# A new constant table of turns for the planner of a one-core hybrid decoder layer

## The chip, the cores and the metric

The kernel runs on one core of a Trainium2 chip. Its time is that of one execution on the device, in microseconds (us); the median of three runs is given. The engines are TensorE (PE, with its weight loads shown apart as PEld), VectorE (DVE), ScalarE (ACT), GpSimd (POOL) and SyncE (SP), which issues the DMA transfers. Each takes its instructions in the order in which the program lists them and waits at an instruction until what it needs is there.

## The reference

One layer of a decoder with two groups of heads side by side, for 1024 tokens of width 1024:

```
h = rms_norm(x)
[a_q a_k a_v a_z a_b a_a | b_q b_k b_v b_z i_q i_k i_w] = h @ w_in
A: q,k,v = silu(causal_conv4(a_qkv)); q,k = l2_norm
   g = -exp(a_log) * softplus(a_a + dt_bias); beta = sigmoid(a_b)
   o_a = rms_norm(gated_delta_rule_chunked(q,k,v,g,beta)) * silu(a_z)      4 heads of 128, chunks of 64
B: score[t,s] = sum_h i_w[t,h] * relu(i_q[t,h] . i_k[s]), causal           8 index heads of 128
   keep the 256 best keys per row; softmax attention on them, QK-normed    8 heads of 64, 2 key heads
   o_b = that * silu(b_z)
x = x + concat(o_a, o_b) @ w_out
gate = sigmoid(rms_norm(x) @ w_ple_gate + b)
x = x + (p @ w_ple) * gate
```

In the chunked delta rule each chunk needs cumulative sums of g, and the inverse of a unit triangular matrix `a_mat`, which comes from solving against the identity. All is float32.

## The kernel before

Products in float32 are made of three fast ones: each operand is split into a high part that the fast format holds and the low rest, and `mm3` (L785) adds high·high, high·low and low·high in one PSUM bank. So a weight block of 128x512 is loaded by a DMA (`raww`), its high part `hiw` is a copy on ACT, and its low part `low` a subtraction on POOL. A 128-column block of the input projection, or of the output projection, takes 8 or 4 weight blocks and is one job of the class Stream. In the trace `hTh` and `hTl` are the split parts of h, `mch` and `mcl` those of the concatenated heads.

The work comes in stages that overlap. First the norm of x and the gate values. `gates` (L1011) computes `g` from the small projection: `gu` on DVE, `nea` (an exponential) and three steps of `ge` on ACT, then two steps of `g` on DVE; then two small matmuls on PE give its cumulative sums and totals, which DVE copies to `gg`.

Then, from about 85 to 540 us, the blocks of the input projection fill PE, and between them run: the index scores; the search of the 256 best keys, bit by bit, on DVE (`topk_v`, L1217, with counts into `junk`) and on ACT (`topk_a`, L1254, counts into `junka`, with small updates on POOL); and group A head by head. For each head `merge` (L1607) builds the inverse of 8 chunk pairs of 128x128 from 32x32 blocks in steps: a product of 64 tiny matmuls, a copy of its result to SBUF (`W0`, on ACT), the next product with it, and so on.

Then the sparse attention, and from about 620 us the output projection. `out_job` (L2011) has four sets of jobs: oA and oB for the first 512 tokens, oC and oD for the others, A and C for the first four weight blocks, B and D for the last four. A job of oD fills one of five PSUM banks (tag `g`), DVE adds the residual from x, ACT squares and copies, POOL adds the squares to `ssum`, and `gate_in` (L2091) or `h2` (L2016) splits the result times the gain for the gate product: high part on ACT, low part on DVE or POOL. `m0Bh` and `m0Bl` are such parts of the second half of the features for the first 512 tokens: the high part is an ACT copy of x2 times the gain, the low part the DVE operation `x2 * g - hi` of L2019, whose two tensor operands both lie in SBUF. `h1Al` is the same for the other tokens, with x in PSUM. The gate product itself (`gate_weights`, `gate_pair`, `gate_last`, L2123 to L2225) uses seven block products in place of eight, which needs sums and differences of weights and of h (`mixl`, `sh`, `sl`, `t1l`), many of them on POOL. The last part of the kernel is this product with its output.

What sets the order is a table. The whole layer is first run against the class Plan (L373), which records each call of an engine as an operation, 7,654 of them, 348 being marks for pools and tiles: 3,873 on PE (a run of small matmuls into one tile is one operation), 1,280 on DVE, 1,075 on ACT, 700 on POOL and 378 DMAs on SP. `add` notes which operation must come before which, by tiles and regions. Buffers are chosen in this recording, so they do not depend on the order. Then `run` (L487) decodes the constant string `TURNS` (L76): entry k is the position, in the list of operations not yet taken, of the one that comes next.

```
for k in raw[:len(ops)] + 256 * raw[len(ops):].astype(int):
    o = ops[left.pop(k)]
    assert all(p in seen for p in o.pre)
```

`issue` (L536) writes the instructions in that order; each is tied to the one before it on its engine, so the table is the program order of every engine. All instructions are issued by one line, so all carry L556 in the profile, and groups are told apart by the names of their tiles.

Of the kernel before, what the change touches and what calls it, by code (L numbers as in the profile page):

```python
# [20 lines left out]
T = 1024  # L21
D = 1024
# [25 lines left out]
_o = 0  # L48
# [24 lines left out]
RG, SG = 3, 3  # L73
# [7 lines left out]
Nug69t5L3%BSFw9wOW-%qf)3;qEab{q8JH;g-|Gj<bi-7BqSiY&nI~0GLK-F$?R66Of(_ALd(n5b}>P%=4~pKMWv$kN=`J1YEdsLMNuO`sa64nWKM(%xr$|3;5N$T22Rim
P(~{mPRq$T6({3(PA-=Vl#F9Jj&m{^hGG7UkxWqvyTYKjqtGZ6DuqIneAZsl(n?AtR|;~4LP5v{nFP`(^(AyX!Ldq~6{Ue>EXzsPMclW^5iHZ!$1ofzRkAcg(=@dR#|Kbe
Uiq$s%J01UH-wS+!4JRl<8Oca-S4TD^6xvo-_-ui@Be_~4Mr247+BJPuWalesDG&W%1@l0uiNlny54sEBFpuaul=LT^=6g}xBNLC$BlT}t2iFTUkMu{Mx!xkyrT^maQx|K
a2)sCQsKB`0bjuJtNb&#ng0@hf#-S6Ii4%zPMzZLIvf{@a6A*w$jG=Pbto)}73?gE#|z^5@x00S(Rjs7MMcGU#U<%)1kc8^mK@9~Syxh0f^RvxrFa70+&?a%Xl&P5#^~yi
# [2274 lines left out]
```

## Time and profile before

| what | value |
|---|---|
| median of three runs | 832.26 us (831.86, 832.26, 835.58) |
| profiled execution | 835.29 us, span 833.3 us |
| mean granted clock of PE | 0.984 |
| PE busy | 811.9 us (97%), 5063 instructions |
| DVE busy | 664.9 us (80%) |
| ACT busy | 589.6 us (71%) |
| POOL busy | 540.9 us (65%) |
| DMA | 93.14 MB |

The span is the part of the profiled execution in which instructions ran. A line of the timeline gives the start, the duration, the engine, the line, the operation, `out<-in` by the program's names, the shapes and a count; in brackets stands how long the engine had stood idle before, and what it waited for. Matmuls overlap in the pipeline, so the time that one costs is read between the starts of two, not from its duration. The clock is the share of full speed granted to PE. The page's clock row and engine rows cut the span into 40 slices of 20.8 us and give tenths.

### The profile page before, as it was taken

The page shows a single profiled execution, that of the slowest core. Times are in us where ns is not written, and L with a number is a line of the kernel's source. Part 1 is how long each engine was busy: PE and PEld are TensorE (multiplying, and loading weights), DVE is VectorE, ACT ScalarE, POOL GpSimd, SP SyncE. Part 2 cuts the span into 40 slices and gives each one's busy share as a digit, 9 for nine tenths or more (in the row PEclk, how much of TensorE's full clock was granted, in tenths as well). Part 3 has the DMA queues.
Part 4 walks back from the last instruction along what each step waited for, and adds up shares of the span by engine and source line. Part 5 has one row for each costly group of instructions (what it writes and reads, how often), then busy time and mean ns, then how long its engine had stood idle before and what let it go on. Part 6 is the DMA issues. An engine that isn't in the chain of part 4 may idle for free.

```text
span 833.3 us, 14829 instructions
## 1 busy us (share of the span) xinstructions
PE 811.9 (97%) x5063; PEld 692.2 (83%) x5063; DVE 664.9 (80%) x1475; ACT 589.6 (71%) x1345; POOL 540.9 (65%) x704
## 2 busy tenths in 40 slices
PE   9998999999999999999999999999999999979996
PEld 6996999987888888888888888878888888768885
DVE  3698757888999999998768854699998786586676
ACT  5765466667999989999775543499886678765342
POOL 3487667524876677577748545368675647988982
PEclk9998999999999999999899999999999999989999
DMA  8963421001122233113312332676313421522453
GB/s 276 371 241 103 159 85 64 1 13 52 39 70 62 89 84 106 58 52 96 87 52 76 87 91 70 219 218 209 113 51 103 155 71 53 197 94 64 140 172 130
DMA packets 77868, 93.14 MB, mean 112 GB/s; under 512 B 24000, under 2 KB 40672, under 8 KB 77664
## 3 DMA queue, kind: packets, MB, share of 16 engines
q1 hardware_dynamic: 77792, 92.20, 34.4%
q8 instruction: 39, 0.64, 0.3%
q14 instruction: 37, 0.30, 0.1%
HBM read 66.72 MB, written 25.45 MB: 111 GB/s over the span
## 4 chain that ended last, share of the span: by engine, by line
PE 80%; DVE 9%; ACT 6%; issue 2%; DMA 1%; POOL 1%; SPq 0%; DVEq 0%; ACTq 0%
PE mm L556 44%; PE g L556 8%; PE lg L556 6%; PE s L556 5%; PE pv L556 4%; PE S L556 4%; PE pt L556 3%; PE c L556 3%; PE rec L556 2%; ACT junka L556 2%; PE po L556 2%; DVE c L556 1%; DVE xT L556 1%; DVE score L556 1%; DVE g L556 1%
## 5 line engine op out<-in xcount | busy, mean ns | idle before, releaser
L556 PE MATMUL mm<-hThi,hiw 128*128 128x512 f32 x400 | 156.8, 405 | 0.6 <-ACT fst L556 0.3
L556 PE MATMUL mm<-hTlo,hiw 128*128 128x512 f32 x400 | 156.3, 402 | 0.0
L556 PE MATMUL mm<-hThi,low 128*128 128x512 f32 x400 | 155.4, 401 | 0.0
L556 POOL TENSOR_TENSOR low<-raww,hiw 128x512 fp32r<-128x512 f32 (+1 forms) x93 | 123.7, 1335 | 43.0 <-ACT hiw L556 26.4
L556 ACT ACTIVATE junka<-score,nt 128x768 bf16<-128x768 int16 (+5 forms) x96 | 99.7, 1039 | 2.5 <-POOL scr L556 0.4
L556 PEld LDWEIGHTS mm<-hThi,hiw 128*128 128x128 f32 x400 | 75.8, 191 | 14.9 <-ACT fst L556 0.7
L556 PEld LDWEIGHTS mm<-hThi,low 128*128 128x128 f32 x400 | 75.9, 190 | 13.9
L556 PEld LDWEIGHTS mm<-hTlo,hiw 128*128 128x128 f32 x400 | 75.8, 190 | 13.6
L556 POOL TENSOR_SCALAR P<-P,rsum 128x128 f32<-128x128 f32 (+7 forms) x64 | 49.1, 773 | 38.0 <-DVE rsum L556 37.4
L556 DVE TENSOR_SCALAR_CACHE_REDUCE junk<-score,cand 128x384 bf16<-128x384 f32 (+2 forms) x96 | 71.1, 740 | 1.3
L556 ACT ACTIVATE hiw<-raww 128x512 fp32r<-128x512 f32 x91 | 56.7, 627 | 19.8 <-PE g L556 8.5
L556 POOL TENSOR_SCALAR nt<-acca,upa 128x1 f32<-128x1 f32 x96 | 36.8, 385 | 40.7 <-ACT junka L556 36.7
L556 ACT ACTIVATE relu<-lg 128x384 f32<-128x384 f32 (+1 forms) x80 | 41.1, 523 | 28.3 <-PE lg L556 24.6
L556 DVE SCALAR_TENSOR_TENSOR score<-relu,sm,score 128x384 f32<-128x384 f32 (+5 forms) x42 | 48.9, 1177 | 11.1 <-ACT relu L556 10.9
L556 ACT ACTIVATE P<-P,mn 128x128 f32<-128x128 f32 (+7 forms) x64 | 49.4, 773 | 11.8 <-DVE mn L556 11.4
L556 DVE TENSOR_TENSOR pl<-pt,ph 128x512 fp32r<-128x512 f32 x72 | 48.3, 685 | 8.2 <-ACT ph L556 6.7
L556 PE MATMUL S<-kst,qT 128*128 128x384 f32 (+2 forms) x192 | 52.3, 354 | 0.3 <-DVE mn L556 0.2
L556 ACT ACTIVATE ph<-pt 128x512 fp32r<-128x512 f32 x72 | 40.9, 594 | 10.4 <-PE pt L556 8.1
L556 ACT ACTIVATE fst<-mm 128x512 f32<-128x512 f32 (+2 forms) x61 | 29.9, 502 | 17.6 <-PE mm L556 17.3
L556 PE MATMUL pt<-ident,P 128*128 128x128 f32 x288 | 40.8, 274 | 0.3 <-POOL P L556 0.2
L556 PEld LDWEIGHTS S<-kst,qT 128*128 128x128 f32 x192 | 34.2, 189 | 7.0 <-DVE mn L556 1.5
L556 DVE SCALAR_TENSOR_TENSOR acc<-fst,cw,acc 128x512 f32<-128x512 f32 x48 | 38.7, 819 | 1.1 <-ACT fst L556 0.4
(434 smaller groups left out, 2507.3 us busy)
## 6 DMA issues: line engine op xcount, KB each, us to landing
raww<-in_w_ct_dram SPq DMA_DIRECT2D x50, 256.0 KB, 2.7
raww<-in_w_out_dram SPq DMA_DIRECT2D x32, 256.0 KB, 3.9
xt<-in_x_dram SPq DMA_DIRECT2D x8, 512.0 KB, 6.4
xc<-in_xc_dram SPq DMA_DIRECT2D x8, 512.0 KB, 7.1
pled<-plt SPq DMA_DIRECT2D x16, 256.0 KB, 4.7
rawi<-in_w_ct_dram SPq DMA_DIRECT2D x16, 256.0 KB, 2.9
pld<-pled SPq DMA_DIRECT2D x16, 256.0 KB, 2.6
out_dram<-gth SPq DMA_DIRECT2D x15, 256.0 KB
```

What stands on the lines that cost most here:

```text
L556: r = getattr(getattr(self.nc, o.eng), fn)(*[real(x) for x in args], **{k: real(v) for k, v in kw.items()})
```

## The change

The string `TURNS` is replaced. The recorded operations, their buffers, their predecessors, `run` and `issue` are as before. It is described as a new table of turns, searched with the duration that each operation had in a trace and with a model of the port that DVE and POOL share. The core of the diff:

```
@@ -74,78 +74,78 @@
 
 
 TURNS = r"""
-c-rlH2Yg(|dFRZ$UiR(2?Y%c(8-N8Ci{6RCf)1h*od5{1q7ftk0tDE=PKu<&B8t605~)H-BrRD<B-u(NpJhw&xy5oj=aNf)@z1t$J}16=U}Rg>Maf+fAOF9_+u5C&Z@&57
...
 """
```

Some 72 such lines of text go and as many come; they cannot be read as they stand. Decoded against the recorded operations, both tables are orders of the same 7,654 entries. Counted on each operation's own engine, the place of 3,405 operations on PE changes, 1,031 on DVE, 872 on ACT, 534 on POOL and 276 on SP. By more than 20 places move 318 on PE, 24 on DVE, 18 on ACT, 16 on POOL and 4 on SP. Of the operations that the prediction speaks of:

| operation | place on its engine, new against old |
|---|---|
| `gu` and `nea * -1` (DVE), L1024, L1018 | 8 and 11 earlier |
| `nea` exponential (ACT), L1017 | 19 earlier |
| both steps of `g` (DVE) | 3 earlier |
| copy of `w0` to `W0` (ACT), L1621, heads 2 to 4 | ahead of the mask operation `score<-eq`, behind one count of `junka` |
| `m0Bl` (DVE), second and third of four | 5 and 21 earlier |
| `low` of the weights of oD3 and oD4 (POOL) | behind two sums of gate weights that they stood ahead of |
| last 13 us of the kernel | unchanged on all engines |

More of the change, by code (lines that the diff above doesn't have):

```diff
@@ L81 @@
[L81 to L84, printed above, removed]
@@ L146 @@
[L146 to L148 removed]
+c-rlG2Y4LUb?&{>?##~a?C$K&&TQ`;i?+a`_ufG?q7eWA0z@G}uoD0)zz(oeETGuICQ78bWJ#t~Y^vDGv%lDJiJjP%9p%M-dGGlpv7DFpl7VE)RG}>=PQH8!|L@zmclNe9
+=bn4ce`Wyq4O&9s%*-O#*tMv!A17Ky7I#G`w6Sj^J^bjSk3Fu~$ZmY>i6@_V>X|#rJI_7;52`o+Uj3sVlN!=w=I!2IM>sCt6|g%RZax0wQ_sHe(l@^Ot#5zl&dc#uU;#l8
@@ new lines @@
+2n2xN4}3o0^#YII1Ke)lb_HE7zsu+Gx&kh@+vNdHm&@gJx&?>R>5MoW4iE}Do$XHF!dQpLvB*(xtFzbI95oJ`y&`C<u=)M|BAc(k2lD(@89A9&t31@|a3ss6HQwP!vf4v-
+;BZ)g&2Ix%ht&n-4o;)PXt!HzHjCA0$uwqw^aV(1Mq8>07hOiD7#}Z23V_XKbBdzRXBRQM$tehe&1STkEEbd5Y&4lnMx!9bVp3|VNr*-zW0HU+7~*B<t@^M&q<7*vol|Eu
+V1mF)#)TogQIsSpP2xq$U@%0ZQ3Ga*2pXM67t#fTd?0{%eOiad<8f=<b}bfXw`#0mD`)XqEFO!+DVMCpqPD0NT9eiyvKk|&)~j`Dpy5+_jaKW|LXAAXnsFEmR*ti9oRL!k
+rAgp8k>fcTYAvVHD7c_fWmYQRQp#|%di|?*y~3q1E3}eUYtU-7I<24uf=;j1X?UKO|IpC1-cGA%rA4WxjSI7JoQ~t<$>fVxtLD@)zQU?TM^!3To|NO1D!E`-844Mmdr)27
@@ new lines @@
+_>PRmAHQS$$xq+2{_NeqmT0r_Z-k$9_y64cbDFpR;0J$cwW%WU6>S}zzL6DeC%bNZ?|a|>35}cx<=GMXC-ij-`XzcBWg?WGDk7AkM{oQ!N=C2fbQu3aNY=#jT0+x4qJC06
+qITYPsom-}_4TW2o4QAR`C^T^y7O$cnIunFT&}1((OmTs*+?EC4J31rVP?p}!`g!Kf&#K(>Pd1DMUh)bl03MLtRyQoR#aT5$j&ayE?reRQ(8(+PL@ne92y=k*|ce7<Hn&4
+8#WAPRcBRgWhyf(zMfuAZd_89UYcG~(wbhJUc?kOq!py)ldJM#xyh9|LpeF6IXO8fJG-eVyRk9WP?A+IgQ}~mBWqXI*4Ad$4A#`-kR(l$Wo4+8Eb$d5ld)J|jHIae<b=*7
+GBI&wBq0({({bT&BwSNNR##V(*|sb)lg#j^lWF-Wd89WbyDT|Np(r8~$atq<w}(Px&_?>p<<df$3(cf##iY?lNEUZYA`C>bJxNMTBoa)r6%!F-G>#<2poet3Ng*IOcs;4p
@@ new lines @@
+nJJygWHnJd(i*&8wMV1ZIG@*O)MT7B9L^!LLs=F}z>=1h#>LXpW1LB0G^Qj)70Hs67%wTrFv|)Gzh0qO#kaeCV0baZFirB0q8XYtRhimFqqw+iutjWcrY(ks216Gu2<^4C
+f&mxw2=S#l9nT}AL1-mXsgN?5rbNq>EJAKK!=Mg%5;}kwM0;q4q1}4D9_eg4WMvo=q9rbyLn;~}<Vs1=Xpoxb*g}<T)=DkXXn2<8SPoewC2cVHTrLA+c+SAs1-(9~4+I#-
+$14rIC@{2Mr_&*xH}dbpz0J+L5OR#m)5@l9S}IGt;2n^J#1>>gf*=Y81Fdh@(}*AD`Q>^&-<PMWtJCo{3()Bdy7vXzph5D}<>jelj36Y7B&&r%vP509#Tt%=<$FZ?B#EZI
+e%XBp?>i)6To4u(Muv%nwO(`6NT*ApZSwXY6jmdVGsrV*R4V!4bBN=DdX-MccpMJiu2fnz7A4Dhy<VfyZA6ko`T&t#!C;UMZddvj)QMck?OdvLI%Tiya3EwG8d47qa@IyG
@@ new lines @@
+XEq~bl%X_9My0YyiDYdn^t`Mctxl&!#l;#_Sh(OI5K=8j<XaGlWgQHP&~Yd%OB6&j9Teqd<gJyZv(so{dl-p923kORgI-qO!WAJM(k{3rPWE$1tx>CyQl(bOeukhF3qFQo
+8A{%9*^UrehW1f=5k*m5l>GdZtQ=;Zxh$_lvrw*&E!1dSfl(wv1ko>_a595L1Vs^)Tus0TDh^_yForL{?l5qp%ny)C_H;O>`M*q8f4^)zfuP)0vSi1>qsNY2fAr0_zWTNQ
+kLm2`xlKnNdG*i8l)~MA{{44;@>lQvid5U|4rgLz|Mnx#zw(|g5KBwTuW#;Lx_0xH7tEIBp4JXl)uvhSv%CuPD}5BlJ*jjPw^Zz-O63hs`G!ULn(|79(xCpLTA!iTOL|fE
+%Sp1^w_&_RmnFMsLExNvO|op27I`C$nP#&YnypAaOnUiv^MZAo)heP^pE<`&nQR1UR5>NbGC^ar89MaELThUWxk@xhlAH9n>Pgno=O8xN37gZ&WH?GgMB%=|;>N<FqDn3h
@@ new lines @@
+2yxlQvOwTifbjWbGv$;@n|+TeB{i3b5>a+hl3A-IVhW8qNns7>n~oLvgK8q#Z-d(sR27@e>)pX1?p!ZRxzdDtTJSi9YXz}=gdJw__3PI=Tt_9h7k4vG)fm$<Dvq3Y>(x%Z
+L+9=@xeR)pU9yRfTUX;=gLx$@^9fR~@%f(h;gdGpJ?B2{)~5sugRkL9fuSMCV9xOH**AtQ`H1h=Wm;}qj!6z3sYT1L!T~d`>mwgq_N9ctBk^e<Mo=lwbN~i#eYw}Wlt@nQ
+daJj0ckeQVtry?A^h*N?)J;op<n7FB!^5jBV~G~(Q20^HijXDfTI>om|Ea6j)e8q*Jv}aWm;0`=v(wqtMJ|cHy<~}FwA0(=E$e(OVk|*l3Li01wKd)1n_^X9ArNndlao8X
+b!OKN_x5m8xKY&*dXuitU-Xq9kB<k}ZoD2YfHk4ZY}Ge|tJqQWHx(8Ba$lLE^v9(rP!TLIuMDJ`|C#LwvIEIPlD~layOg|qcRuWZ?H#UmWt%I~3f(O&Mb6e%%;EPn<whqJ
@@ new lines @@
+yfsNSF*zKEYAmT$+A1umva-@vrLN4Pm~us>(NuoGzS?NR*t-tzmkYk@h?T}l0-&hWo~1HngA6B#<QTK<w&IYjkOukH?ImuYGA=IvMHFBm31n}x3YjnmlzWOT#lU8It{zJI
+ZM<m<4<`XQy4eqk<E_?6gazhcmRU0R6}A_KO|64qwQ-E|hJg5$5dc;QBh|yeJX|^C)>X)a&;*=C?wB#vu{{N(N+4<jNe({2PDLV0O$5Y=VRc6*=%5RPH3fGILadM@u$cpH
+T`tJ^i?lP@-5@tN*O8OsNX=T&?*(7WVBX3|(zsLIz^Q#lNB07aI!m1yHhm|Z1;(^AApQ4LF_!wec=s;IeLZSne(_~DOqeuL3chG*3b2I|uwc*>2r<S0rVogJ=1=ltA^+De
+i`N3!)BaxwPevX##>Jh9;@?K1<y3<C|C~5O&HZ3D^0m|GXQ_PBx1-T4HzL!Wx?jaI2Qpm>D&0w@`_jl*fzO-w|4{Bvoo^Nt1l9S$hPXw}_{3!*a@g$>*+r4Fvu?D1_w4Rj
@@ new lines @@
+7+4A%`CG_cq;1zOH`&qA;X?nIpZ}x$yPg$F50kCe;n*4--rQ`BH8O(!mpJdB`&m4`7g>6k=?YIdBcze*5w1%q$iRyrDr{C83371d%0XjJEm5mx`Z9apSljz}R;BfS;6FW~
+p>U(7>mXhPI*o-2Ld;7Kvmt_1=(2+Uo5^6Rv^6B1x>`$@Q|eNxtn621YATT-$w*`=8`u4FwxlFn>|+bRv$&1;$JW5&c0BLz^8C3BPHGuklO9CjR4w9&q+j}r@uCWXD=)9l
+#Os(kFjZTNh0WEW(z<~<td{rJg5>Hk3L{t#W{Bbd2fV7fSt<PUy1>##p({y9t^<h))JUc=Uf6-@PS(N`$tQ3DuReiSRYmaH!v_v(XGdnQP?^=sHCCD~f0#CN)lXM%u2wWR
+H+#627Or_*`{E{Hqjr;aqh-UB+=i|7ys4I-KUOpLBD^RDgaHp!+<d*kHRtLFH%A|duTP02c!4$?N-ue}w{iE<65trk4;RMe2Il|N)|q|L){ekUkf`x^0B_9t?khB%b21TB
@@ new lines @@
+3dbTxkC%KE=*x~4eZREmz=0H?Yxrh^3Dm#9RMks|x({aL%t{AZrJ0#;Sq@nac8TRP>0$7{U>F`g+>(<*!@rt=;2lt>+msl2F1`sAEB@9Q8j7YQXp^t-iHTQXDopL0UEAkK
+`A)1SW{mxPY$O&NjK!cjmGeg7=DR82CsD8#_=wf3kEf20CvAE!`;ZZAp9R~t?Gx5D9c|%SO5>Ex#13M6qcvxGx?$?<FvF@CMx{q3oB7Fkt#aL4m)_LcmG<>#$8DP|x~13`
+UopRIR^Q2a?X|0G*15C;Yp9p3!+(1x|IQt1+33W?m4=DUp3S#6PVQ0<RqVXtn=YAFPX!(wL3)pAvMq>A#)#kVd&r0%lPLFGPU@IAJ~KY9A0MZp8x@N6&1?1@(9n$u6t#bN
+R8_0pNfA?qb!X0~=FV`-xxvBQ^>T4!h&$L%s&z@Eu)MUQiYp%B`lfnzOz$7;?buH8s?bTYs4#C+?XAfj7aNt#IpWIMwTj-&{M01BdD~_lQ#ENWH5wY$8P+@3)jRjsvYE$g
@@ new lines @@
+$?7V_q3Ipur77!<hj&?*TUV5hG+Kx3Bh2s>+t8!7^|p2OYZ>eO>6hoL#;n`p$gT7Ra-{2Q(?owTP>i?X-T3OBvF<fb9JqM0=Y;f7{<_nrji;WNKZT1|MhusSsi7@b&VONa
+v~=Z#l@u5msjNOb!YWy|A1j$J!4y-|(-n&ClZ$6S*OtAoqjaWYfBwE1xc}PzAO3Le>R&dz`|i8?cPZwlQ2ox+y8Z7wRDJFkx$EevI(WGDd+@t828cl&Sq6!<e8c*Nv2UO$
+_$TDsJN~5Z?QPpa+Ye4`uidtH?}&Q$_JeBMY}L%x15;fyGZ5SM#*-MQ=2|&^<tr4AK~{6kaaEz(0acA#tGCqClat4S69D8gD&Xi<0w-Wq3b0}%d*ryyVON8+#wO6f1PhLD
+h^|-UuS=()3NG81EUu_XfGjrLn2~Y&HkNiP{r2tK5v*6|n1D;6-LA312y9ni_V)kTzPPQr<3QZya_ka&5xb<g*nR<HE?{-%GS2y~4_wn>SK#%8T2~F!)NHBIRM%>1>~q3t
@@ new lines @@
+oAnH)KV8V5EOS(?s<KucYtl6~o-^prp5>&A7cX-B<rZ!80+0R+r0?xROAUl@q^(*IzyXV3UMyA`n&dQoQK=vvEUqzbE}4|fjpBGgzF6Pg)6>~i&P!_!6wMB`@1Jd-S+u{6
+J$$$owH;t)XGdpR4abfxKRPKqd-(X_r!FwmxpM~(_3C<gU9WMevB!9+ySv-iWA5xSFEMv@b?y46eO)`R?cBe!YwzCdDRU?0T;xm-)YhgCZwm|sh6{&=uCE!owx)hHcG*90
+k-l)jx9oh<$jHOKGv{SW6BrCE9~~Wq&#m;YSmM8a-9HqR1H$$FfqnY|m-mMH`a-9&PoIXT!Y5CLyS9awY&jA>+IeJhOXudzU~)f53#Ne$q4agmSSH~7W83^7Jr)x{Upm~7
+vJ0+Lu3HBqad0fW8ecI60RV#|cE#9xW9^Vxb;dUey(_#;!1=SDPSE88y?)FGAn<}FPphX%)r>$0kf09uaNwzxeRd52s$iiM4@(WX`9*QCDGVDzixxps0Ga{xL`4`~Fi<$e
@@ new lines @@
+MIsz@z=xo%2X@DBR*5T;_NU@<Tl3B&J=~##Myyr~gPKZ@U#oY?IYprs%Xe#XZE}vUQHzihI9!F>lpJnW#c_Twu5{yGFLd!vhXQJ%8uXac>`(*FCwV#UQUbst(BTL@?_>k4
+o%MQcti{EeITIT)ssbupsqnb;E>^+g<D}JM0SK9q2_Yb2G}QAdfUC7?pav>A2x%{a3Jrq+)x+o?M&{5pbQR%%yhPm~wV8lOr-|GP#CedNU4$3n1$A|2>grl?oWPrK;>eK(
+@MR3c<lqC^+uPrN@5a8LpJ57xQOz5*?y$`bw2?@BG^e1jqH1yLs<rDLyY&?xgas(ydLZv)PhR(-LwN^JFb^#mMD)PGo&nT9v-5EKGL;HYl;Wkm6a#n3S=i2n6j;57+>Lgr
+lzP2Fr6MnCDDs?Qk*c1g93--_YzoPp;*OKd(TJ!ygjf;;C^^X&ky>a)`W7OAsNklFdcvrbTw1NdV{cH{>Xmg06=7o3YNNx!CK!!nR!;0D^t3*oLb-1#S_pL~ucyc`PYQ%S
@@ new lines @@
+-zN|TNemlw<@Wakf>3D+*#eiFFiQ^3W=uzEmTWSMqJ?xS%^Bk<3MD7&)QLm_Y0?;p)R0AOl`<}=y#}?YG$hY)b{R>r3}>+&x;^m;Hy(L?<^V5kIQkwzXhS|Z2MH!ITpAN|
+5_GtbR#+1#OHMYCOjm{zbzRm}GFt*!cxDFCm`Lae9T83?;>~!JjH;8giFky!$k~2CfxAlh9L+!!`81kr+@8saPID-UP?07{CH_$9$~Mq!$ZOX#K2hN@6c*EBN-R}~W@klx
+f_Jf*w#U<SY>}C#4XH6@iaRROC2TN6OL4ST!!RzuR}uNE+;-9Vs}f3SPf${n3g$SKj--GljrIvbINwrLjiZEeWp-9c7ETq437Qz5)33t)$xC%az|3lkii-E8XQq48*cdA&
+h&5tlDwdSUN~Kj*oKRUQloKW|LFBd-62WY*i2Jkr2FgQ4+FILNTQf6TA{iN*aePr48CujBuCGraYAKu^AI+$5sEifUw3m)ca+lU7*436I<`pI87G^F@>?!UEcXyE?oFGH4
@@ L149 @@
+pC9{djP=8bu+K(yKcRQ*4`aojg$4gs*pF!$yT26oGqX=Iv`=T{*zel>PaLy99+`(9J<-3*Q^P;RH~u?>N%-jz8a~JsKCcwy^9t<ODHo2*nG{9+N9rE_akmQoS2vpfa^B~`
+S$?3d2lzdk{=wV-2Y7%7__yO<04TP;%K
 """
```

88 lines of the change are left out of this document (20 added, 68 removed).

## The prediction

> **What bounds the kernel now.** I read the page first, then the waits of PE by releaser, then the stretches where the granted clock is below 1, then the timelines around each.
>
> ```profile
> span 833.3 us, 14829 instructions
> ...
> PE 811.9 (97%) x5063; PEld 692.2 (83%) x5063; DVE 664.9 (80%) x1475; ACT 589.6 (71%) x1345; POOL 540.9 (65%) x704
> ...
> PEclk9998999999999999999899999999999999989999
> ...
> PE 80%; DVE 9%; ACT 6%; issue 2%; DMA 1%; POOL 1%; SPq 0%; DVEq 0%; ACTq 0%
> ```
>
> TensorE is the bound: 97% busy, 80% of the chain that ended last. A new order leaves its 5063 instructions as they are, so it can win only what is not matmul at full rate: waits of PE, and slices where its clock is low (the 8s in the clock row).
>
> ```profile
> PE g L556 <- DVE t1l L556: 3.4, 1, 3.4
> PE mm L556 <- DVE g L556: 2.2, 1, 2.2
> PE s L556 <- ACT W L556: 2.2, 3, 1.4
> ...
> PE mm L556 <- DVE gg L556: 1.2, 1, 1.2
> PE mm L556 <- ACT sh L556: 1.0, 1, 1.0
> PE g L556 <- POOL low L556: 1.0, 1, 1.0
> PE rec L556 <- DVE r L556: 0.4, 1, 0.4
> ...
> PE mm L556 <- ACT fst L556: 0.3, 1, 0.3
> ```
>
> These rows sum to 11.7 us, and one wait is over 3 us. Three stretches run at half clock:
>
> ```profile
> 75.62:82.44 6.82, 5.66 (x17) 5.19 (x18) 5.99 (x12) 5.01 (x9) 2.94 (x3) 0.50 0.00 1
> 410.13:420.37 10.24, 9.94 (x119) 8.45 (x120) 5.01 (x8) 7.83 (x20) 6.78 (x13) 0.50 0.24 79
> 741.22:748.04 6.82, 5.95 (x14) 4.69 (x15) 6.16 (x9) 4.65 (x9) 6.66 (x6) 0.50 0.20 74
> ```
>
> The columns are length, then busy time of PE, weight load, DVE, ACT and POOL, then clock. What half a clock costs is seen in two pairs of starts of the same 512-column matmul:
>
> ```profile
> 737.85 0.39 PE L556 MATMUL g<-mch,low 128*128 128x512 f32 x1
> 738.08 0.39 PE L556 MATMUL g<-mch,hiw 128*128 128x512 f32 x1
> ...
> 743.11 0.63 PE L556 MATMUL mm<-m0Bh,sh 128*128 128x512 f32 x1
> 743.54 0.63 PE L556 MATMUL mm<-m0Bl,sh 128*128 128x512 f32 x1
> ```
>
> The cadence goes from 0.23 to 0.43 us, so about half of a stretch is lost: 6.82/2 = 3.4, 10.24/2 = 5.1 and 3.4 us, 11.9 in all. The three starts lie 334.51 and 331.09 us apart, 98 and 97 times 3.413, and the lengths are 2, 3 and 2 times that: the clock changes on a grid. Waits and slow clock together are 23.6 us, the most that a better order could win here; each stretch begins beside one of the waits, so both fall together.
>
> **The change, part by part.** Nothing is removed and nothing added: every engine runs the same operations on the same buffers. Decoding the two tables gives the moves: 3,405 of PE's 3,873 operations change place, but only 318 by over 20 places; on DVE 1,031 of 1,280, on ACT 872 of 1,075, on POOL 534 of 700, of the DMAs on SP 276 of 378. The last 13 us are in the same order. I cost the places where the waits above stand.
>
> *Gates (71 to 82 us).*
>
> ```profile
> 73.71 0.41 PE L556 MATMUL mm<-g,tri 128*128 128x32 f32 x2 [2.25 <-DVE g L556]
> ...
> 76.78 0.69 PE L556 MATMUL mm<-hThi,si 128*128 128x384 f32 x1 [1.20 <-DVE gg L556]
> ```
>
> ```profile
> 71.38 1.06 DVE L556 SCALAR_TENSOR_TENSOR g<-gu,ge 128x32 f32<-128x32 f32 x1 [1.16 <-ACT ge L556]
> 72.47 1.18 DVE L556 TENSOR_TENSOR g<-g,nea 128x32 f32<-128x32 f32 x1
> 73.58 0.69 DVE L556 TENSOR_TENSOR c<-c,hThi 128x512 f32<-128x512 f32 x1
> ```
>
> PE waits for g, a chain of small operations through ACT and DVE. In the new table gu stands 8 places earlier on DVE, the exponential for nea 19 earlier on ACT, the ge steps 3 to 4 earlier, and both g operations 3 earlier, while the cumulative-sum matmul keeps its place among PE's work. The DVE operations that g passes are like the one at 73.58, three of 0.69 or some 2 us; g would be ready at about 71.8 instead of 73.6, and 2.25 falls to about 0.5: **−1.7** (bounds 0 and −2.25). The 1.20 behind it stays: the copy of gg still stands four DVE operations behind, with the same few matmuls between. The stretch of half clock that began at 75.62 had both waits in it; with one left I take it as gone, **−3.4** (bounds 0 and −3.4). What is late next is that copy, 1.20 us as now.
>
> *Merge of the third head (408 to 421 us).*
>
> ```profile
> 410.43 1.05 PE L556 MATMUL s<-U,W 32*32 32x16 f32 x64 [1.38 <-ACT W L556]
> ```
>
> ```profile
> 408.15 1.51 DVE L556 SCALAR_TENSOR_TENSOR eq<-score,cand,eq 128x384 bf16<-128x384 f32 x1
> ```
>
> ```profile
> 409.69 0.52 ACT L556 ACTIVATE score<-eq 128x384 f32<-128x384 bf16 x1 [1.83 <-DVE eq L556]
> 410.12 0.26 ACT L556 ACTIVATE W<-s 128x128 f32<-128x128 f32 x1
> 410.28 1.14 ACT L556 ACTIVATE junka<-score,nt 128x1024 bf16<-128x1024 f32 x1
> ```
>
> The copy W that PE waits for stands on ACT behind the score operation, which itself waits 1.83 us for DVE's eq. The new table puts the copy ahead of it, but behind a junka count (1.14 us), and gives PE 0.65 us of other work between the two small products, for this head and the next; for the first it stays at none. So 1.38 falls by 0.65 and the 0.52 of the score operation, less what is left of the count: **−1.0** (bounds −1.38 and +1.14, the copy held by a whole count). The half clock from 410.13 follows this wait and the small products before it; gone, **−5.1** (bounds 0 and −5.1).
>
> The Trainium skill, "TensorE: Matmul & The Clock Gate", section "Why this matters for your kernels", wants no PE gap over about 3 us, since one whole idle window puts the clock to half. Here 1.38 us was the longest gap before 410.13, so the trace does not agree that it takes a whole idle window; by the page neither the first two stretches nor any like them would follow from waits this short.
>
> *Tail (715 to 760 us).*
>
> ```profile
> 717.47 1.32 DVE L556 SCALAR_TENSOR_TENSOR m0Bl<-x,g,m0Bh 128x512 fp32r<-128x512 f32 x1 [0.68 <-ACT m0Bh L556]
> ...
> 732.54 0.74 DVE L556 SCALAR_TENSOR_TENSOR h1Al<-g,g,h1Ah 128x512 fp32r<-128x512 f32 x1
> 733.20 4.79 DVE L556 SCALAR_TENSOR_TENSOR m0Bl<-x,g,m0Bh 128x512 fp32r<-128x512 f32 x1
> ```
>
> ```profile
> 734.86 1.32 POOL L556 TENSOR_TENSOR low<-raww,hiw 128x512 fp32r<-128x512 f32 x1
> 736.12 1.32 POOL L556 TENSOR_TENSOR low<-rawg,hiw 128x512 fp32r<-128x512 f32 x1
> 740.54 1.27 POOL L556 TENSOR_TENSOR sl<-mixl,sh 128x512 fp32r<-128x512 f32 x1 [3.10 <-ACT sh L556]
> 759.84 1.30 POOL L556 TENSOR_TENSOR ssum<-ssum,mixl 128x512 f32<-128x512 f32 x1 [2.19 <-ACT mixl L556]
> ```
>
> ```profile
> 720.00:740.00 20.00, 16.27 (x72) 12.30 (x70) 14.28 (x16) 14.89 (x28) 17.44 (x14) 1.00 0.36 119
> ...
> 760.00:780.00 20.00, 20.00 (x94) 16.30 (x93) 12.13 (x19) 9.83 (x17) 20.00 (x17) 1.00 0.38 120
> ```
>
> m0Bl, the low part of a half of h for the gate, took 4.79 us where h1Al of the same shape took 0.74 and another m0Bl 1.32. m0Bl reads two SBUF operands, h1Al takes one from PSUM; it ended at 737.99, 0.55 us after POOL's run of low operations ended at 737.44. So this DVE operation gets in only where POOL has a gap. Behind it on DVE stood t1l, hence PE's 3.4 us and the half clock from 741.22. The new table moves this m0Bl 5 places ahead, to about 724, and another 21 ahead, to the one at 717; it also has the weights for the fifth step of the output projection come with 8.7 us of PE work ahead of their use, not 2.5. PE's loss here is 3.4 + 1.0 + 1.0 + 3.4 (half clock) = 8.8 us, but POOL is full at 760 to 780 and PE then lives from hand to mouth, so the gain cannot pass what POOL was idle: 3.10 + 2.19 = 5.3 (the other gaps are under 1 us). I take **−4.0** (bounds −5.3 and, with the block recurring, 0; the slower end is a rival below).
>
> The Trainium skill, "SBUF — State Buffer", section "SBUF: two separate sides", calls the port that VectorE and GpSimd share an exclusive lock that whichever starts first holds for its instruction. By that a moved m0Bl would cost one POOL operation, 1.3 us, wherever it stands, and the tail −5.3. The trace does not agree: two POOL operations that began at 734.86 and 736.12 went ahead of a m0Bl issued at 733.20.
>
> *The small waits.* The rows fst (0.3), r (0.4), and the rest of W (2.2 − 1.38 = 0.8) have 0.65 to 6 us more PE work between producer and user in the new table: **−1.3** (bounds 0 and −1.5).
>
> *What the new order adds.* No row shows it. Between nothing and as much as the present order has in waits, 11.7; DVE and ACT are the tight engines from 200 to 400 us, where most of the wide moves are. As nine in ten PE operations move by no more than 20 places I lean below the middle: **+5.0**.
>
> **Sum.** −1.7 −3.4 −1.0 −5.1 −4.0 −1.3 +5.0 = −11.5. The profiled execution took 835.29, its span 833.3 and 2.0 around it; 835.29 − 11.5 = 823.8. The runs' median is 832.26 and the slowest 835.58: 3.3 apart, about one half-clock stretch of 3.4, so the sum's first stretch may be what the median already lacks, and I do not take it off twice. **Forecast 824 us**, −1.0% on the median.
>
> **Rivals.** *The clock goes free.* If no short wait is left that meets the grid and the added waits stay at 1.5 us in place of 5 with the tail at its −5.3: 824 − 3.5 − 1.3 − 2 (the remaining 1.20 at the gates covered) = 817. For it: the only full stops are those named. Against: 1.38 us was enough at 410. It is also what follows from the Trainium skill, "TensorE: Matmul & The Clock Gate", section "Why this matters for your kernels", once the one wait over 3 us is gone.
>
> *New waits eat the gain.* The sum's 11.7 of new waits, one of them at the grid (3.4), and a half clock at 410 that stays (5.1) make 823.8 + 6.7 + 3.4 = 834 with the first stretch, or 831 on an execution without it; I put it at 832. For it: a table in which 3,405 operations move has as many chances of a late producer as this one. Against: the larger waits above each have their own cure in the moves.
>
> *The block comes earlier and longer (slower).* m0Bl at about 724 stands at the start of POOL's dense stretch, 17.44 busy of 20 us from 720, ended at 737.44. If POOL leaves no gap, m0Bl is held from 724 to 737.99, 14.0 us and not 4.79, and everything on DVE behind it: the additions that free PE's five banks for the output projection. PE goes on until its banks are full, then waits. Against the forecast that costs the 4.0 not won, some 9.2 more held less the 2 us that the banks carry, 7.2, and another window of half clock, 1.7: 824 + 12.9 = 837. It passes the median when m0Bl is held over about 4.8 + 4.3 = 9 us. For it: 717.47 ended just where two POOL operations depended on one another, the only sort of gap there was. Against: the new order also sets such a dependent pair for POOL near 724, and one gap is enough.
>
> **How the numbers follow.** Forecast 0.48, free clock 0.18, gain eaten 0.21, block longer 0.13. The range 813 to 835 takes 4 us below the free clock for the bounds of the waits, and ends short of the last rival. The forecast's own range is 819 to 828. About 0.5%, 4.2 us, is what a measurement of this kernel can tell from no change, so faster means below 828.1: the first two cases, 0.66; the same, 0.20; slower 0.14.
>
> **What would show it.** In the waits of PE: the rows for t1l and for g gone or under 1 us, W under 1 us; the clock row without its 8s at a tenth, a half and nine tenths of the span; m0Bl under 2 us in each of its four runs. POOL gapless through 720 to 790 would show that the tail has nothing more to give. Wrong would be: half-clock stretches of the same sum at other places; an m0Bl over 5 us; or PE waits that again sum to over 10 us with new names.

## The result, and the profile after

The median goes from 832.06 (four runs now, one more than above) to 818.66 us, 13.4 us off; the ratio is 0.9836 with a 95% interval of 0.9802 to 0.987. Timed again in a later set it was 0.9848 (0.9822 to 0.9874). The profiled execution took 819.22 us against 835.29.

The page of the new kernel, the same rows as before:

```profile
span 817.5 us, 14817 instructions
...
PE 801.5 (98%) x5063; PEld 683.0 (84%) x5063; DVE 658.3 (81%) x1475; ACT 587.7 (72%) x1345; POOL 542.9 (66%) x704
...
PEclk9999999999999999999999999999999999999999
...
PE 85%; POOL 5%; ACT 3%; DVE 3%; DMA 2%; issue 2%; SPq 0%; POOLq 0%; DVEq 0%
```

The three 8s of the clock row are gone; PE stands on 85% of the last chain in place of 80%. Its waits, by releaser, longest first (`issue` means that the profile shows nothing that it waited for):

```profile
PE mm L556 <- POOL sl L556: 2.7, 2, 1.8
PE xT L556 <- DVE ident L556: 1.5, 1, 1.5
PE mm L556 <- ACT score L556: 1.3, 1, 1.3
PE s L556 <- issue: 1.2, 1, 1.2
```

All rows of this view summed to 14.7 us before and to 9.8 now. So of about 16 us less in the profiled execution, 4.9 are waits, and most of the rest is the half clock, which cost 11.9 before by the prediction's estimate and nothing now before PE's end.

These two executions are not typical ones, though. Every timed execution has its own mean granted clock: 0.982 to 0.995 in 69 of the kernel before, half of them at 0.989 or less, and 0.993 to 0.999 in nine of the new one. The two profiled ones had 0.984 and 0.999, near the two far ends. With half of the time at half clock counted as lost, that is 9.4 us on average before and 4.0 now, PE's end included, which is at half clock in both kernels. By this estimate the half clock gives 5.4 of the 13.4 us between the two averages, and the larger part was lost at full clock.

Where on PE the time went can be told by its work. For each matmul I took the time to the next start, less the cadence of that size at full clock (0.227 us for 512 columns, 0.108 for 128, and so on), and added this up over PE's work, which is 769 us in both kernels:

| stretch of PE's work, us | lost before | lost now |
|---|---|---|
| 0 to 60, norm and first weights | 6.5 | 8.5 |
| 60 to 70, gates | 7.1 | 0.5 |
| 70 to 380 | 11.9 | 9.2 |
| 380 to 390, third head's merge | 7.8 | 1.0 |
| 390 to 670 | 11.8 | 15.8 |
| 670 to 720, output projection and gate weights | 10.3 | 4.8 |
| 720 to 769 | 0.8 | 0.9 |
| all | 56.1 | 40.6 |

At the gates, PE's timeline and DVE's in the new kernel:

```profile
73.08 0.40 PE L556 MATMUL mm<-hThi,hiw 128*128 128x512 f32 x1
73.31 0.30 PE L556 MATMUL mm<-g,tri 128*128 128x32 f32 x2
...
74.92 0.34 PE L556 MATMUL mm<-hThi,si 128*128 128x384 f32 x1
```

```profile
68.37 0.56 DVE L556 SCALAR_TENSOR_TENSOR g<-gu,ge 128x32 f32<-128x32 f32 x1
...
70.32 1.14 DVE L556 TENSOR_TENSOR g<-g,nea 128x32 f32<-128x32 f32 x1
...
73.18 0.69 DVE L556 TENSOR_TENSOR c<-c,hThi 128x512 f32<-128x512 f32 x1
73.88 0.23 DVE L556 COPY gg<-mm 128x64 f32<-128x64 f32 x1
```

The first step of g no longer waits for ACT. g was ready at 71.46, the sums were taken at 73.31 without a wait, and the copy of gg came 0.4 us after them, so the product with si did not wait either.

At the third head's merge, PE and ACT:

```profile
404.05 0.72 PE L556 MATMUL s<-T,NB 32*32 32x16 f32 x64
404.71 0.49 PE L556 MATMUL rec<-vnew,kh 128*128 128x128 f32 x2
...
405.57 0.72 PE L556 MATMUL s<-U,W 32*32 32x16 f32 x64
```

```profile
404.83 0.28 ACT L556 ACTIVATE W<-s 128x128 f32<-128x128 f32 x1 [1.15 <-PE s L556]
405.01 0.51 ACT L556 ACTIVATE score<-eq 128x384 f32<-128x384 bf16 x1
```

The copy goes ahead of the mask operation, and PE has other work between the two tiny products.

In the tail, DVE's m0Bl, and POOL around it:

```profile
717.27 1.93 DVE L556 SCALAR_TENSOR_TENSOR m0Bl<-x,g,m0Bh 128x512 fp32r<-128x512 f32 x1
```

```profile
717.38 1.28 POOL L556 TENSOR_TENSOR sl<-mixl,sh 128x512 fp32r<-128x512 f32 x1
718.60 1.75 POOL L556 TENSOR_TENSOR mixl<-mixl,rawg 128x512 f32<-128x512 f32 x1
```

m0Bl is let in after one POOL operation, and ends 0.60 us after 718.60. It takes no gap: POOL's next operation starts before the last one's recorded end, and is longer, 1.75 and not 1.3.

### The profile page after: what moved, and what is told of

It is laid out like the page before. It is cut to its first block, busy times and chain, and to the rows that moved or that the text cites. A ratio compares the mean times of both kernels' runs of the same rounds, so it can differ in the third digit from the quotient of the medians.

```text
span 817.5 us, 14817 instructions
## 1 busy us (share of the span) xinstructions
PE 801.5 (98%) x5063; PEld 683.0 (84%) x5063; DVE 658.3 (81%) x1475; ACT 587.7 (72%) x1345; POOL 542.9 (66%) x704
## 4 chain that ended last, share of the span: by engine, by line
PE 85%; POOL 5%; ACT 3%; DVE 3%; DMA 2%; issue 2%; SPq 0%; POOLq 0%; DVEq 0%
PE mm L556 49%; PE g L556 7%; PE lg L556 6%; PE s L556 5%; PE pv L556 4%; PE S L556 4%; PE pt L556 4%; PE c L556 3%; PE rec L556 2%; PE po L556 2%; POOL low L556 1%; ACT P L556 1%; DMA xc<-in_xc_dram 1%; POOL ssum L556 1%; POOL mixl L556 1%
## 5 line engine op out<-in xcount | busy, mean ns | idle before, releaser
L556 POOL TENSOR_SCALAR nt<-acca,upa 128x1 f32<-128x1 f32 x96 | 39.0, 408 | 36.7 <-ACT junka L556 32.7
L556 ACT ACTIVATE relu<-lg 128x384 f32<-128x384 f32 (+2 forms) x80 | 41.3, 524 | 26.8 <-PE lg L556 25.1
L556 DVE SCALAR_TENSOR_TENSOR score<-relu,sm,score 128x384 f32<-128x384 f32 (+5 forms) x42 | 49.2, 1183 | 12.1 <-ACT relu L556 11.8
L556 PE MATMUL S<-kst,qT 128*128 128x384 f32 (+2 forms) x192 | 54.2, 359 | 0.6 <-DMA kst<-kd 0.4
L556 PE MATMUL pt<-ident,P 128*128 128x128 f32 x288 | 44.4, 273 | 0.3 <-POOL P L556 0.3
L556 PEld LDWEIGHTS pt<-ident,P 128*128 128x128 f32 x288 | 35.1, 141 | 7.9 <-POOL P L556 1.1
```

What stands on the lines that cost most here:

```text
L556: r = getattr(getattr(self.nc, o.eng), fn)(*[real(x) for x in args], **{k: real(v) for k, v in kw.items()})
```

## The experiments

All orders are given as the decoded lists, since the table itself can't be read. Ratios are to the kernel before, timed on the same chip in the same set. Operations are counted from 0.

**Three parts, each alone.** The two orders have done exactly the same set of operations at the 5,049th and at the 6,734th, so they can be joined there; at the 937th they differ by four operations each way.

```diff
 front:   - old[0:937]                + new[0:937]      then old
 middle:  - old[937:5049]             + new[937:5049]   between old parts
 tail:    - old[6734:]                + new[6734:]
```

> New order for the first 937 of 7,654 operations (to about 91 us of the profile before), then the old order. If the parts stand for themselves, this keeps what the new table's trace shows up to there: PE loses 4.5 us less than before at the same point of its work (2.0 more by 60 us, 6.6 less at the gates), so a ratio of about 0.995, and the half-clock stretch near 76 us is gone. Rival: half-clock stretches only move with their grid, and the time is that of before (ratio 1.000).

> Old order for the first 937 operations, new order from there to the 5,049th (about 534 us, where both orders have done the same set), old order behind. By the traces PE loses 6 us less in this part, 6.8 of it at the third head's merge and its half clock: ratio about 0.993. Rival, that the wait for the score mask comes back when the front is late by 4.5 us: no gain, 1.000, with the half clock near 410 us still there.

> Old order up to the 6,734th operation (about 706 us, where both orders have done the same set), new order behind. By the traces 5.0 us less lost in this part: ratio about 0.994, the m0Bl of 4.8 us down to about 1.9, no half clock near 741 us. If instead the tail is bound by POOL whatever DVE does, no more than the 1 to 2 us by which POOL's own gaps shrink: ratio 0.998 or above.

Measured: front 0.9933 (0.9912 to 0.9955), middle 0.9951 (0.9928 to 0.9974), tail 0.9937 (0.9912 to 0.9962). The three add up to 1.79%, the whole table gives 1.64%, and none of the three rivals holds. In the profile of the front the half clock near 76 us is gone. In that of the tail the second m0Bl took 1.93 us, as with the whole table, but one window of half clock is left at 730 us, behind a wait of 1.8 us for sl; none was expected.

The middle's 6 us were 4.1, and not all of them need come from its own place. In its profile PE lost 0.9 us at the third head's merge, as expected, but also only 4.8 at the tail, which has the old order there, and not the 10.3 of before: m0Bl took 1.03 us, as is shown below. So part of what the tail's moves give can come without them, and the three parts do not quite stand for themselves.

**One pair on POOL.**

```diff
 POOL, order of before, about 731 us:
  low
- mixl<-v,mixl     (third sum of gate weights)
- sl<-mixl,sh      (second sl)
+ sl<-mixl,sh
+ mixl<-v,mixl
  sl<-mixl,sh      (third sl, of the third sum)
```

> The order of before with one pair of neighbours on POOL exchanged in the tail: the second sl now stands ahead of the sum of gate weights it stood behind, so that the third sl follows directly on the operation it depends on, at about 733.6 us. DVE's order is that of before. If DVE gets the shared port only in a gap that two dependent POOL operations leave, m0Bl issued at 733.2 ends at about 734 to 735 (1.0 to 1.9 us and not 4.8), PE's wait of 3.4 us for t1l goes and the half clock at 741 us with it: 4 to 6 us off, less about 1.3 by which the exchanged sum is late: ratio 0.994 to 0.997. If the port goes to whichever starts first, or m0Bl is slow for another reason, it stays at 4.8 us or so and the ratio is 1.000 or a little above.

The ratio is 0.9969 (0.9946 to 0.9992). DVE and POOL:

```profile
732.48 1.26 DVE L553 SCALAR_TENSOR_TENSOR m0Bl<-x,g,m0Bh 128x512 fp32r<-128x512 f32 x1
```

```profile
731.93 1.27 POOL L553 TENSOR_TENSOR mixl<-v,mixl 128x512 f32<-128x512 f32 x1
733.94 1.29 POOL L553 TENSOR_TENSOR sl<-mixl,sh 128x512 fp32r<-128x512 f32 x1 [0.74 <-ACT sh L553]
```

With DVE's order untouched, m0Bl goes from 4.79 to 1.26 us because POOL now stops at 733.20, and PE's wait for t1l is no longer in its list. So POOL held DVE there, as the prediction read it. PE paid with a wait for the late sum (`PE mm <- ACT sh`, 2.5 us in place of 1.0), and one window of half clock, from 734.48 to 737.89 us, is left behind that wait.

**m0Bl alone, five places earlier.**

```diff
 DVE, order of before:
  h1Al<-g,g,h1Ah
  r<-mm
+ m0Bl<-x,g,m0Bh   (second)
  ...              (nine operations)
- m0Bl<-x,g,m0Bh
  h1Al<-g,g,h1Ah
```

> The order of before with one operation moved: the second m0Bl on DVE stands five places earlier, as in the new table, at about 723.3 us by the trace of before; POOL's order is that of before. If DVE gets the port only where POOL stops for a dependent pair, the next such pair is the one at 728.6, m0Bl takes 5 to 6 us, what stands behind it on DVE (the additions for oD0 and oD1) is that late, and PE waits: ratio 1.000 to 1.005. If POOL's operations let it in at the next change from one to the next, it takes 1.3 to 2 us, PE's wait of 3.4 us for t1l and the half clock at 741 us are gone: ratio 0.992 to 0.996.

0.9946 (0.9924 to 0.9969): the theory that DVE gets in only where POOL stops falls. DVE and POOL:

```profile
721.41 1.05 DVE L553 SCALAR_TENSOR_TENSOR m0Bl<-x,g,m0Bh 128x512 fp32r<-128x512 f32 x1
```

```profile
720.60 1.31 POOL L553 TENSOR_TENSOR mcl<-mixl,mch 128x512 fp32r<-128x512 f32 x1
721.87 2.99 POOL L553 TENSOR_TENSOR mixl<-rawg,rawg 128x512 f32<-128x512 f32 x2
```

m0Bl got in at 721.87, where POOL went from one operation to an independent one, and ended 0.59 us later; the pair of POOL operations took 2.99 us in place of 2.55. This one move gives 0.54%, nearly all of the tail's 0.63%. (It stood nine recorded operations earlier on DVE; five is the difference against the new table, where other operations moved too.)

**m0Bl 0.7 us later.**

```diff
 DVE, order of before, about 733 us:
- m0Bl<-x,g,m0Bh
  h1Al<-g,g,h1Ah
+ m0Bl<-x,g,m0Bh
```

> The order of before with one pair of neighbours on DVE exchanged: the second m0Bl stands behind the h1Al that followed it, so it is issued about 0.7 us later, at 733.9, with POOL's three operations of 733.6, 734.9 and 736.1 as before. If the run of back-to-back POOL operations shuts it out, it ends again at about 738.0 (4.1 us), and the ratio is 0.999 to 1.000. If the 4.8 us come of the moment at which it was issued, 0.3 to 0.4 us ahead of POOL's next operation, it now gets in at 734.9 and ends at 735.5 (1.6 us), PE's wait for t1l goes and with it mostly the half clock: 0.993 to 0.996.

0.9996 (0.9974 to 1.0018). DVE and POOL:

```profile
736.24 3.60 DVE L553 SCALAR_TENSOR_TENSOR m0Bl<-x,g,m0Bh 128x512 fp32r<-128x512 f32 x1
```

```profile
734.26 2.53 POOL L553 TENSOR_TENSOR sl<-mixl,sh 128x512 fp32r<-128x512 f32 x2
736.75 1.29 POOL L553 TENSOR_TENSOR low<-raww,hiw 128x512 fp32r<-128x512 f32 x1
738.00 1.29 POOL L553 TENSOR_TENSOR low<-rawg,hiw 128x512 fp32r<-128x512 f32 x1
```

It was passed over at 736.75 and 738.00 and ended 0.55 us after POOL's run, so issuing it later did not help. (In this profile PE waits 2.7 us for t1l, across the border of two windows, and no half clock follows in the tail.) What stands on POOL matters, then. But it is not the list of operations alone either: with the middle part of the new table in front, the tail has both queues' old order, and yet

```profile
727.02 1.03 DVE L553 SCALAR_TENSOR_TENSOR m0Bl<-x,g,m0Bh 128x512 fp32r<-128x512 f32 x1
```

```profile
726.22 3.00 POOL L553 TENSOR_TENSOR sl<-mixl,sh 128x512 fp32r<-128x512 f32 x2
```

here it got in between the two sl, the second of which passed it over in the kernel before. Nor is it how long before POOL's next change m0Bl is issued: 0.4 us in the kernel before and 0.51 in the run with m0Bl later, where it was passed over, 0.46 and about 0.45 where it was let in at once. What makes POOL let DVE in at one change of operations and not at the next is left open.

**The copy of w0 alone.**

```diff
 ACT, order of before, about 408 us:
+ W<-s          (copy of w0, third head)
  score<-eq
- W<-s
  junka<-score,nt
```

> The order of before with one operation moved: on ACT, the third head's copy of w0 now stands ahead of the score mask operation that waits for DVE's eq. PE's order is that of before, so it still has nothing to do between the two tiny products. If a short wait inside one 3.4 us window is what halves the clock, PE's gap of 1.9 us there falls to about 0.6 and the half clock near 410 us goes: 1.3 + 3.4 to 5.1 off, ratio 0.992 to 0.9945. If the tiny matmuls themselves bring the half clock, it stays: 1.3 off, ratio 0.998 to 0.999.

0.9982 (0.9962 to 1.0003). In the profile the place does what was expected: the wait is 0.39 and the clock stays whole. PE's product with the copy, and two windows:

```profile
411.77 0.40 PE L553 MATMUL s<-U,W 32*32 32x16 f32 x27 [0.39 <-ACT W L553]
```

```profile
401.00:411.00 10.00, 9.80 (x88) 8.03 (x89) 8.07 (x17) 8.52 (x23) 6.44 (x9) 1.00 0.41 105
411.00:421.00 10.00, 9.47 (x230) 8.20 (x218) 7.76 (x16) 9.13 (x22) 8.32 (x12) 1.00 0.30 104
```

PE loses 2.9 us there, not 7.8. The timed runs show only 1.5 us, with an interval that ends at 3.2. Six profiles that have the old merge (before, front, tail, POOL's pair, both moves of m0Bl) all have a half-clock stretch there, of 3.4 to 10.2 us, so that there is one is no chance of one execution, but its length varies. The granted clocks of the timed runs fit the small gain: by the estimate of the section on the result they lose 6.9 us to half clock, the kernel before beside them 8.9, so 2.0 us less where the profile of before promised 5.1. At which place these 2.0 were won the timed runs cannot show.

**Half clock on purpose.** The new order, with 17 extra waits put on PE:

```diff
 issue(), after the instructions of o:
+ if o.i in HOLD:
+     self.tc.add_manual_dep(o.ins[0], self.ops[HOLD[o.i]].ins[-1].name, mybir.DependencyInfo(
+         mybir.DependencyClass.Sync, mybir.DependencyReason.DATA), reason="hold")
```

> The new order with 17 holds added: a matmul of PE, about every 11 us between 95 and 200 and between 565 and 700 us, also waits for an operation of DVE, ACT or POOL that ended 1.3 to 3.1 us later in the new table's trace. The matmuls around are full ones. No hold is over 3.4 us. If the clock goes to half after a window of the 3.413 us grid in which PE stood still for over about half of it, most holds of 2.2 us or more bring a half-clock stretch and those of 1.4 nearly none, and the windows ahead of half-clock stretches are the ones with the most idle time, whatever the longest gap. If a whole idle window is needed (the Trainium skill, 'TensorE: Matmul & The Clock Gate', section 'Why this matters for your kernels'), there is no half clock anywhere after the start. Time about 818 + 20 to 35 for the holds, and up to 1.7 more for each half-clock window.

858.26 us in one run, at the upper end of what was expected, and two half-clock stretches. Three windows of the grid (each 3.41 us) and what followed the first:

```profile
210.45:213.86 3.41, 0.52 (x3) 0.31 (x3) 1.72 (x4) 1.65 (x5) 2.06 (x3) 1.00 0.00 0
213.86:217.27 3.41, 3.41 (x10) 2.67 (x9) 2.54 (x8) 2.27 (x4) 1.65 (x3) 0.50 0.00 0
620.04:623.45 3.41, 1.51 (x10) 1.02 (x8) 1.48 (x5) 2.92 (x6) 2.93 (x3) 1.00 0.16 34
...
493.75:497.16 3.41, 2.08 (x43) 1.79 (x42) 0.61 (x2) 1.44 (x7) 2.00 (x5) 1.00 0.00 1
```

PE's longest stop in the first window was 2.89 us, with 0.52 us of PE busy, and the clock was halved. A stop of 2.42 left 1.51 us busy in the window at 620, and it was not. Six holds stopped PE for 2.2 us or more and one of them was followed by half clock, so "most holds of 2.2 us or more" was wrong. The second stretch began after 493.75 with no hold near it: 43 matmuls, most of them the tiny ones of a merge, and no gap over 1.33 us. Put together over all 14 profiles of this case, with the cadence time of matmuls of more than 32 columns as a share of each window after the first 15 us (and windows already at half clock left out):

| share of the window in full-size matmuls | windows | next at half clock |
|---|---|---|
| 0.25 or less | 16 | 16 |
| 0.26 to 0.38 | 32 | 8 |
| over 0.38 | 3,179 | 0 |

Of the 24, 19 had a longest wait under 2.5 us inside the window. Some in the middle row that kept the clock had many tiny matmuls beside, so these seem to count in part. With the tiny ones counted in full the share tells the windows apart less well: some of up to 0.65 were followed by half clock, and others from 0.39 on were not. The bounds of the table were chosen on these same windows and have not been tried on others. A whole idle window is not needed, which is what the Trainium skill, "TensorE: Matmul & The Clock Gate", section "Why this matters for your kernels", gives as the cause; the grid of 3.413 us that the same page states is what every trace here shows.

**Eleven moves on the old order.**

```diff
 ACT:  + nea exp, 8 places earlier; ge, ge, ge 5 earlier
 DVE:  + nea * -1 and gu, 7 and 4 earlier; first step of g 2 earlier; copy of gg 3 earlier
 ACT:  + copy of w0, third head, ahead of score<-eq
 POOL: + second sl ahead of the third sum of gate weights      (first version)
 DVE:  + second m0Bl behind r                                  (second version)
```

> The order of before with only eleven operations moved: at the gates nine (on ACT the exponential for nea and the three steps of ge, on DVE nea, gu, both steps of g and the copy of gg), the copy of w0 for the third head on ACT, and the pair of neighbours on POOL in the tail. If the three places of the prediction carry the gain, it is 2.2 + 1.2 + 3.4 at the gates, 4.7 to 6.4 at the merge, 2.6 as measured for POOL's pair: 13 off the profiled time, ratio 0.985 to 0.988, as much as the whole new table. If the gain is spread over the thousands of other moves, less than half of it: 0.993 or above.

> The order of before with eleven operations moved, as in the run with eleven, but in the tail the second m0Bl on DVE (five places earlier, which by itself gave 0.9946) in place of POOL's pair (0.9969 by itself). If parts add, 0.990 - 0.002 = 0.988, about 0.7 of the new table's gain with 11 moves of some 6,800. If the moves hide each other's gain, 0.990 or above.

0.9902 (0.9883 to 0.9922) with POOL's pair and 0.9875 (0.985 to 0.9899) with m0Bl. (The second step of g, counted among the eleven, kept its place, so ten operations moved.) The first run lies between its two expectations: the three places carry 0.98%, not all of the gain. In the second version they carry 1.25%, against 1.52% for the whole table in the same set, and no half clock before PE's end is left in its profile. So ten moves give about four fifths of what the table gives, which changes the place of 6,118 operations. By their clocks the timed runs of the second version lose 2.0 us to half clock, the new table in the same set 4.2: what the other moves add was won at full clock.

**The new table's own waits.**

```diff
 PE, new order, about 716 us:
+ nine matmuls of oD3 and oD4
  g<-mch,low (oD4)
- mm<-mch,sl            waits 1.8 us for sl
+ mm<-mch,sl
 PE about 724 us:  + four of oD5 ahead of mm<-m0Bh,sl (waits 0.8)
 POOL:  + low of the first gate weight ahead of two ssum additions
 DVE:   + one t2f ahead of the addition for oD5
```

> The new order with its two remaining waits of the tail treated: on PE nine matmuls of the output projection whose operands are long there stand ahead of the product that waits 1.8 us for sl, and four ahead of the one that waits 0.8; on POOL one low is put ahead of two additions to ssum, on DVE one sum for the gate one place ahead. If PE sets the time there, 2 to 3 us less than the new table: ratio 0.980 to 0.982 of the kernel before, 0.9965 to 0.9975 of the new one. If POOL, which is without a gap there, sets it, the waits come back behind and the time is that of the new table.

> The new table, timed again beside the others of this call: ratio about 0.984 (interval so far 0.980 to 0.987). Half clock in the profile in at most one place, since its windows come close to a third of full-size matmul time only near 480 us.

0.9872 (0.9847 to 0.9898), the new table beside it 0.9848: nothing won. In the profile PE is 2.0 us ahead of the new table of the same set at 700 us of its work (1.5 of it from before the tail) and has given all of it back by 720; the wait for sl is 0.4 us, in its place stand short ones for sh, a low and t1l, and m0Bl, issued at another moment, took 3.22 us. The windows of the new kernel suggest why, POOL's busy time being the last of the five:

```profile
700.00:720.00 20.00, 18.02 (x82) 14.20 (x81) 12.59 (x16) 14.33 (x26) 20.00 (x16) 1.00 0.51 169
720.00:740.00 20.00, 18.95 (x84) 14.89 (x83) 15.20 (x23) 15.88 (x29) 19.92 (x17) 1.00 0.28 93
740.00:760.00 20.00, 20.00 (x93) 16.22 (x92) 12.55 (x21) 11.92 (x22) 20.00 (x17) 1.00 0.28 86
```

POOL has next to no gap for 60 us there, which fits the second expectation, that POOL sets the tail. It is not shown: in the run with the mended waits POOL is busy for only 18.54 of the 20 us from 720, and m0Bl's 3.22 us are another cause. The new table, profiled again, had one half-clock window past its start, after 480 us, where it was expected.

## Why the prediction came out as it did

It said 824 us, faster; 818.66 lies 5.3 us below, inside the range of 813 to 835 and a third of a microsecond outside the forecast's own range of 819 to 828. The three places and the direction were right, the gain was forecast too small. Term by term, from PE's lost time in the two profiles:

- *Gates*, −5.1 forecast, −6.6 in the profile; the whole front alone gave 0.67%, 5.6 us. That g's chain set PE's wait and the half clock behind it was right, its size was not. The step that failed is "g would be ready at about 71.8 instead of 73.6": it counts the DVE operations that g passes, but not the 1.16 us for which the first step of g stood waiting for ACT in the kernel before, and which are gone. g, which had ended 2.2 us after PE could have taken the sums, now ends 1.85 us before PE takes them. That 71.46 lies near 71.8 is luck, because everything in this execution came later from its start: in the profile of the front alone g ended at 68.61, again 1.9 us ahead of the sums at 70.49. With it falls "the 1.20 behind it stays": in these 1.9 us DVE runs through three of the four operations ahead of the copy of gg, and one is left. (The first step of g stands 5 places earlier on DVE, and not 3 as the table of the moves has it.)
- *Merge*, −6.1 forecast, −6.8 in the profile. Moved by itself, the copy takes 1.0 of the 1.38 us of the wait and the half clock away in the profile; the timed runs gain 1.5, as told above.
- *Tail*, −4.0 forecast, −5.5 in the profile, 0.63% (5.2 us) timed. That m0Bl behind POOL's run set t1l and PE's wait was right: one move, on POOL or on DVE, removes both. The move on DVE removes the half clock too; with that on POOL a window of it is left behind another wait. The bound of 5.3 by POOL's idle time was about reached. Wrong was "gets in only where POOL has a gap": with the move alone it got in where POOL had none. The row that should have warned is DVE's eq at 408.15, 1.51 us and so ended at 409.66, beside POOL's rows of before:

```profile
407.64 1.60 POOL L556 TENSOR_TENSOR low<-raww,hiw 128x512 fp32r<-128x512 f32 x1
409.21 0.51 POOL L556 TENSOR_TENSOR rs<-rs,f 128x4 f32<-128x4 f32 x1
```

By its end it seems to have got in at 409.21, behind a low with no gap after it.

- *Small waits*, −1.3 forecast; the whole stretch from 70 to 380 us lost 2.7 less.
- *Added waits*, +5.0 forecast as a leaning between bounds; 2.0 at the start and 4.0 between 390 and 670 us came, 6.0. Of the start, the wait for the bank that ACT's copy to score frees (1.3 us) hung on a late DMA; in the profile of the front alone it is absent, with the same order up to there, so this part is chance. Of the 4.0, 1.2 are the wait `PE s <- issue` near 478 us; the rest was not followed up.

The sum was −11.5 and the profiled execution fell by 16.1; the medians fell by 13.4, since the profiled execution of before stood 3.2 above its median and that of the new one 0.6. The text had seen that difference and did not use it, which happened to cancel part of what the terms lacked. It is luck in another way too that the terms come so near: they compare two executions whose clocks lie near the two ends. The half clock, 11.9 us in the profile of before, gives 5.4 by the estimate over all timed executions, and the 8.0 us left for the work at full clock are more than the terms for the waits have. The 23.6 us called the most to be won counts 11.7 us of waits; all rows of that view sum to 14.7, and PE's lost time to 56.1.

Of the rivals, "the clock goes free" at 817 is nearer in time than the forecast, and in the profile it is what happened: no half clock before PE's end. That was chance. The other eight timed executions had clocks of 0.993 to 0.996, and the second profile of the new table has a window of half clock at 480 us: the matmuls near 477 us filled 0.33 of a window of the grid in the first profile and 0.22 in the second. In the experiments too half clock came back behind waits of 1.0 to 2.9 us. And what was added came to 6, not 1.5. "New waits eat the gain" took 11.7 us of new waits. Its sum is wrong as well: it names the half clock of 5.1 that stays, but 823.8 + 6.7 + 3.4 leaves it out; with it the sum is 839. Its sign, waits that again sum to over 10 us, was just missed with 9.8. "The block comes earlier and longer" did not happen in any of the four profiles with the new tail's order (1.93 us each); with the moves meant to mend its waits m0Bl came up to 3.22.

## What to carry to other kernels

Where PE is the bound and runs at 97%, look for the stretches in which its granted clock is not 1 as well as for waits: here each of the three stretches stood beside a wait for one late operation. Ask for each what the window ahead of it held, and free the one operation that was late; ten moves gave four fifths of what a search over the whole order gave. But before you price such a stretch from one profile, read the granted clocks of the other executions: here the two profiles differ by 11.9 us of half clock, all timed executions by 5.4 on average. Before moving PE's work in a stretch, see whether another engine runs there without a gap: the waits may then only change their names.

## What the runs showed of the hardware

In the 14 profiles of this case the clock was halved from one tick of a 3.413 us grid to the next when full-size matmuls filled a quarter of the window ahead or less (16 of 16), never when they filled over 0.38 of it (0 of 3,179). A wait of 1.2 us beside tiny matmuls was enough, a stop of 2.42 us among full ones was not.

m0Bl, a DVE operation of 128x512 with two SBUF operands, takes 0.74 us alone. Beside back-to-back POOL operations on SBUF operands it took 1.0 to 1.7 us where it began at POOL's next change of operations, and the POOL operation that starts at that moment takes up to 1.75 us in place of 1.3. The Trainium skill, "SBUF — State Buffer", section "SBUF: two separate sides", describes an exclusive lock for whichever starts first; these cases agree. The 1.93, 3.22, 3.60, 4.72 and 4.79 us do not: there one to three POOL operations that started later went ahead.
